# Splitting the first load of a stream-bound kernel: 512 columns ahead of 15,872

## The chip, the cores and the metric

One core of a Trainium2 chip. The metric is the time of one execution in device microseconds; most executions of a kernel here agree within 0.3%.

## The reference

```python
def reference(x, y, axis):                 # x, y: 1024 x 4096 float32, axis = -1
    return np.sum((x - y) ** 2, axis=axis).astype(np.float32)
```

33.55 MB are read, 4 KB written.

## The kernel before

Each of the 128 partitions holds eight whole rows, 32,768 columns of x and of y. Both are loaded in pieces that get smaller towards the end. VectorE subtracts, ScalarE squares and sums, and the last piece is squared and summed on VectorE.

```python
xv = x.rearrange("(p r) d -> p (r d)", p=P)      # one partition: 128 KB in a row
xw = [16384, 8192, 3072, 2688, 1312, 768, 352]   # columns of each x load
yw = [15648, 8192, 3072, 2688, 1312, 768]        # and of each y load
# ... (pieces of y are also cut out at the end: 736 and 352 columns)

def load(landed, src, dst, name, c0, c1):
    sem = tc.alloc_semaphore("%s%d" % (name, len(landed)))
    nc.sync.dma_start(out=dst[:, home(c0, c1)], in_=src[:, c0:c1]).then_inc(sem, 16)
    landed.append(((c0, c1), sem))

# order: each y load behind as much x as it needs
todo = list(order)
for _ in range(2):
    load(*todo.pop(0))               # the first two loads ...
prog.early(mybir.EngineType.SP)      # ... go out ahead of the start barrier
while todo and todo[0][5] <= H:      # H: 24,576 columns fit the buffers
    load(*todo.pop(0))
# ... compute; later loads wait until ScalarE has freed a row
```

All loads go out from one queue, SP's, and one load runs on all 16 DMA engines: eight partitions, hence eight packets, for each.

Of the kernel before, what the change touches and what calls it, by code (L numbers as in the profile page):

```python
# [52 lines left out]
def kernel(tc, x, y, axis, out):  # L53
# [21 lines left out]



    xw = [16384, 8192, 3072, 2688, 1312, 768, 352]
    yw = [15648, 8192, 3072, 2688, 1312, 768]
    late, last = 736, 352  # L80
    LATE = 3
# [201 lines left out]
```

## Time and profile before

| | before |
|---|---|
| time, median (3 runs) | 86.06 us (86.02 to 86.10) |
| span of the profiled run | 84.1 us |
| VectorE / ScalarE busy | 43% / 38% |
| DMA engines' share | 94.1% |

Three more lines of the kernel before: the packet count from the page and, from the timeline (start, length, engine, instruction), the last subtractions and the store.

```profile
DMA packets 2304, 33.56 MB, mean 399 GB/s; under 512 B 384, under 2 KB 640, under 8 KB 1280
```

```profile
78.52 2.34 DVE L172 TENSOR_TENSOR X<-X,Y 128x768 f32<-128x768 f32 x3 [0.26 <-DMA Y<-in_y_dram]
...
81.71 0.35 SPq L245 DMA_DIRECT2D out_dram<-results  x1
```

VectorE still waits for data at 78.52 us, and the store goes out 3.2 us later: the end hangs on the stream of loads.

The packet count is 2,048 packets of data (15 loads and the store, 128 each) and 256 completion records of 4 bytes, one per engine and transfer.

### The profile page before, as it was taken

How to read it: one execution, taken by the hardware profiler on the slowest of the kernel's cores; microseconds unless marked ns; L12 is line 12 of the kernel's file. 1: busy time of each engine (PE TensorE's matmuls, PEld its weight loads, DVE VectorE, ACT ScalarE, POOL GpSimd, SP SyncE). 2: the span in 40 equal slices, each digit the busy share in tenths (PEclk: the TensorE clock that was granted, in tenths of full speed). 3: DMA queues.
4: the chain of work that ended last, by engine and by line, in shares of the span. 5: the costliest groups of instructions: out<-in, count | busy, mean ns of one | idle time of the engine just before them, and what ended most of it. 6: DMA issues, size and time to landing. Idle time of an engine off the chain costs nothing.

```text
span 84.1 us, 110 instructions
## 1 busy us (share of the span) xinstructions
DVE 36.3 (43%) x17; ACT 31.6 (38%) x26; POOL 0.2 (0%) x4
## 2 busy tenths in 40 slices
DVE  0000000000000000000899999990699999199870
ACT  4200000000000000000007979799505979997980
POOL 0000000000000000000000000000000000000000
DMA  9479999992999999995899979996999999999900
GB/s 499 187 312 499 499 499 499 499 436 92 447 476 476 476 476 476 476 476 249 358 390 499 499 327 421 499 452 296 438 421 438 424 424 425 400 424 412 363 0 2
DMA packets 2304, 33.56 MB, mean 399 GB/s; under 512 B 384, under 2 KB 640, under 8 KB 1280
## 3 DMA queue, kind: packets, MB, share of 16 engines
q1 hardware_dynamic: 2304, 33.56, 94.1%
HBM read 33.55 MB, written 0.00 MB: 399 GB/s over the span
## 4 chain that ended last, share of the span: by engine, by line
DMA 71%; DVE 14%; ACT 10%; SPq 1%; issue 0%
DMA Y<-in_y_dram 71%; DVE X L172 14%; ACT X L178 10%; SPq L114 1%; ACT results L219 0%
## 5 line engine op out<-in xcount | busy, mean ns | idle before, releaser
L172 DVE TENSOR_TENSOR X<-X,Y 128x4096 f32<-128x4096 f32 (+8 forms) x13 | 35.6, 2781 | 45.2 <-DMA Y<-in_y_dram 45.1
L178 ACT ACTIVATE X<-X 128x4096 f32<-128x4096 f32 (+7 forms) x12 | 29.4, 2449 | 48.7 <-DVE X L172 48.7
L178 ACT ACTIVATION_READ_ACCUMULATOR X<-X 128x1 f32 x12 | 2.2, 186 | 0.0
L178 ACT ACT_TABLE_LOAD x1 | 1.3, 1283 | 1.3 <-PEq L264 1.3
L202 DVE CUSTOM_DVE_ANT_0 Y<-X,head 128x352 f32<-128x352 f32 x1 | 0.6, 583 | 0.1
L219 ACT ACTIVATE results<-parts 128x1 f32<-128x1 f32 x1 | 0.3, 294 | 0.0
L196 DVE TENSOR_REDUCE head<-parts 128x1 f32<-128x3 f32 x1 | 0.1, 150 | 0.0
L235 DVE TENSOR_REDUCE results<-parts 128x1 f32<-128x2 f32 x1 | 0.1, 147 | 0.0
L264 POOL MEMSET const-bfloat16-1.0<- 128x1 bf16 x1 | 0.1, 102 | 0.0
L264 POOL MEMSET const-uint8-127<- 128x1 uint8 x1 | 0.1, 102 | 0.0
L264 POOL MEMSET const-float32-0.0<- 128x1 f32 x1 | 0.1, 99 | 0.2 <-issue 0.2
L264 POOL MEMSET const-float32-1.0<- 128x1 f32 x1 | 0.1, 99 | 0.0
L202 DVE DVE_READ_ACCUMULATOR2_ANT results<- 128x1 f32 x1 | 0.1, 81 | 0.0
## 6 DMA issues: line engine op xcount, KB each, us to landing
Y<-in_y_dram SPq DMA_DIRECT2D x1, 7824.0 KB, 39.8
X<-in_x_dram SPq DMA_DIRECT2D x1, 4096.0 KB, 48.6
Y<-in_y_dram SPq DMA_DIRECT2D x1, 4096.0 KB, 58.0
X<-in_x_dram SPq DMA_DIRECT2D x1, 1536.0 KB, 14.9
Y<-in_y_dram SPq DMA_DIRECT2D x1, 1536.0 KB, 18.2
X<-in_x_dram SPq DMA_DIRECT2D x1, 1344.0 KB, 17.5
Y<-in_y_dram SPq DMA_DIRECT2D x1, 1344.0 KB, 20.4
X<-in_x_dram SPq DMA_DIRECT2D x1, 656.0 KB, 21.5
```

The lines of the kernel that those rows point to most:

```text
L114: nc.sync.dma_start(out=dst[:, home(c0, c1)], in_=src[:, c0:c1]).then_inc(sem, 16)
L172: nc.vector.tensor_sub(out=a, in0=a, in1=Y[:, home(c0, c1)]).then_inc(diffs, 1)
L178: nc.scalar.activation(out=a, in_=a, func=Square, accum_out=acc).then_inc(acts, 1)
L196: nc.vector.tensor_reduce(out=head, in_=parts_of(r, len(row_parts[r]) - 1), axis=mybir.AxisListType.X, op=add).then_inc(sums, 1)
L202: nc.vector.tensor_tensor_reduce(out=Y[:, home(*piece)], in0=X[:, home(*piece)], in1=X[:, home(*piece)], scale=1.0, scalar=head, op0=mult, ...
L219: nc.scalar.activation(out=results[:, r : r + 1], in_=b, func=Identity, bias=a).then_inc(acts, 1)
L235: nc.vector.tensor_reduce(out=results[:, r : r + 1], in_=parts_of(r, len(row_parts[r])), axis=mybir.AxisListType.X, op=add,).then_inc(sums, 1)
L264: nc = _bacc.Bacc("TRN2", target_bir_lowering=False, num_devices=1)
```

## The change

The intent, as the size suggests: small packets (2 KB a row instead of 64 KB) should get the stream moving sooner. The diff is one line:

```diff
-    xw = [16384, 8192, 3072, 2688, 1312, 768, 352]
+    xw = [512, 15872, 8192, 3072, 2688, 1312, 768, 352]
```

Because exactly two loads go out ahead of the barrier, the second part of x also takes the early place that the first y load had.

## The prediction

> **What bounds the kernel now.** I read the page first, then the start and the end of the timeline, the table by stages, and the packet records of the trace one by one. The page's busy shares and its slices:
>
> ```profile
> span 84.1 us, 110 instructions
> DVE 36.3 (43%) x17; ACT 31.6 (38%) x26; POOL 0.2 (0%) x4
> ...
> DMA  9479999992999999995899979996999999999900
> ...
> q1 hardware_dynamic: 2304, 33.56, 94.1%
> ```
>
> No compute engine is busy for half of the span; the DMA engines are for 94.1% of it. The dips in the row of slices come from booking long packets in whole slices. The table by stages has columns for the stretch, its length, each engine's busy time, clock, DMA share and GB/s:
>
> ```profile
> 0.00:1.00 1.00, 0.00 (x0) 0.00 (x0) 0.20 (x4) 1.00 0.00 0
> 1.00:40.00 39.00, 0.00 (x0) 1.28 (x1) 0.00 (x0) 1.00 1.02 434
> ...
> 59.00:73.00 14.00, 12.03 (x3) 9.30 (x7) 0.00 (x0) 1.00 1.00 424
> 73.00:80.00 7.00, 6.10 (x6) 6.39 (x9) 0.00 (x0) 1.00 0.98 395
> ```
>
> One unbroken stream from 1.00 to about 80 us. The packet records confirm it: each of the 16 engines moves one packet at a time, each starting where the last ended, with no hole from 1.00 to 79.91 us, and the last load's count is complete at 80.31 us. What follows is fixed: the last subtraction, the fused square and sum, and the store. So **the time is the moment at which the stream starts moving, plus its transfer time, plus a fixed tail**.
>
> The chain of waits seems to say something else and needs care:
>
> ```profile
> 40.21 8.77 DVE X L172 x2
> 48.98 0.02 issue
> 49.01 3.72 ACT X L178 x2
> 52.73 0.02 issue
> 52.74 0.33 SPq L114
> 53.07 0.04 issue
> 53.11 20.36 DMA Y<-in_y_dram
> ```
>
> It goes through compute because the issue at 52.74 waited for a freed buffer. But the first packet of that load (10,752 bytes each) started at 66.21 us: the load stood in the queue for 13 us behind earlier ones. Compute in the middle has that much slack; only the queue counts.
>
> The start, which the change touches:
>
> ```profile
> 0.00 0.38 SPq L114 DMA_DIRECT2D X<-in_x_dram  x1
> ...
> 0.43 0.42 SPq L114 DMA_DIRECT2D Y<-in_y_dram  x1
> ...
> 1.26 0.33 SPq L114 DMA_DIRECT2D X<-in_x_dram  x1
> 1.64 0.52 SPq L114 DMA_DIRECT2D Y<-in_y_dram  x1
> ```
>
> The first issue takes 0.38 us and its first packet is recorded at 1.00 us. The first round of 16 packets of 65,536 bytes then takes 3,109 ns on average (2,596 to 3,316), all later rounds of that size 2,419 ns: the start loses 0.69 us besides the first empty 1.00 us. That is all that a change of the first packets could win. Fifteen engines start between 1.00 and 1.31 us and lose 0.56 to 0.90 us; one starts at 1.78 and loses 0.18. So the loss depends on the moment rather than on the packet: real flow begins about 1.65 to 2.06 us on every engine (ends at 4.07 to 4.48, less 2.42).
>
> **What the Trainium skill says.** "DMA: Bandwidth & Descriptors", section Specifications, puts the ceiling of the 16 engines at 435 GB/s and the first byte of a hardware-generated DMA at about 0.6 us. The trace agrees with both: 16 x 65,536 bytes in 2.419 us are 433 GB/s, and from the end of the first issue (0.38) to the first packet (1.00) is 0.62 us. The stream therefore runs at its ceiling and no shape of packet raises it. The same page, "Why small descriptors are slow", tells of a fixed overhead of about 3 cycles per packet. The trace shows such a constant: the median packet is 2,420 ns for 65,536 bytes, 1,213 for 32,768, 460 for 12,288, 121 for 3,072 and 60 for 1,408. From the first two the slope is 1,207 / 32,768 = 0.03683 ns per byte; what is left over is 6, 6, 7, 8 and 8 ns. "Perfetto Trace Analysis", section DMA Optimizations, warns that DMAs under 2 KB pay significantly per transfer; here the 1,408-byte packets of the tail pay 8 of 60 ns, and 2,048 bytes sit at the edge. The first page's section "Latency and other measured facts" has HBM access at 0.2 us on average and 2 us under high load; the 0.69 us lies between, but no record here shows what it consists of.
>
> **The change part by part.** The order of instructions per engine is the same on all but SP, which has one DMA more: x in 512 columns, x in 15,872, then y in 15,648.
>
> Bytes stay: 33.56 MB, 0 us. Packets rise by 128 (one per partition) from 2,304 to 2,432, which is 8 more per engine. A row of 65,536 bytes (2,420 ns) becomes one of 2,048 bytes, 0.03683 x 2,048 + 8 = 83 ns, and one of 63,488, 0.03683 x 63,488 + 6 = 2,344 ns: together 2,427, or 7 ns more. Eight rows make 8 x 7 = 0.06 us per engine on the path. One completion record of some 9 ns more per engine makes it 0.07.
>
> Issue: the first one should still take about 0.38 us, since its length doesn't follow the size (0.33 to 0.52 for loads of 4 to 8 MB), so the first packet comes at 1.00 again. The second part of x takes y's early place at 0.43 and reaches the engines about 1.43. The small packets last until 1.65 + 8 x 0.083 = 2.3 us on the earliest engine, so no hole: spare 0.9 us. Y now goes out behind the barrier at about 1.26 and is needed when x ends at 21 us: 19 us to spare, no cost. All later issues slip by one place, some 0.4 us, against 20 us of queue.
>
> Start loss of 0.69 us: I choose to leave it as it is. An engine that can't get data before about 1.65 to 2.06 us can't get it in small packets either, and the read wait is then paid once, in the first packet or spread over the first few. Change: 0.
>
> VectorE waits for one semaphore more before its first subtraction. That count will be complete near 1.65 to 2.06 + 0.66 + 0.35 (the delay from last packet to landing, 21.39 to 21.74 in this trace) = 2.7 to 3.1 us, against 40.2 us, and the middle has slack: 0 us.
>
> Sum: +0.07 us. Last landing 80.31 to 80.38, span 84.1 to about 84.2, time 86.06 to 86.13, rounded to **86.1 us**.
>
> **The rivals.** (A) The slow first round belongs to the large packet, for example 16 engines reading long bursts at once from a standstill; small first packets would take the edge off, and the big ones would follow with their reads already under way. For it: only the first round is slow, and the shift to y at 21 us, as cold an input as x was, costs nothing (2,309 ns from its first round on) because it starts behind running packets. Against it: the engine that began latest lost least with the same 64 KB packet. At the most it wins the 0.69 less 0.07, 0.6 us, giving 85.5; half of it gives 85.8. I give it 15 to 20%.
>
> (B) Small packets from a standstill each expose part of the read wait, or many rows at one column offset hit the same part of the memory. Against it: in the tail five loads of 3,072 down to 1,408 bytes per row, all 128 rows at one offset with the same 128 KB pitch, run at exactly the rate of the fit, to the nanosecond. They had running reads ahead, though. If the eight packets took 0.1 us more each, the loss would be up to 0.8 us where nothing hides it; since the big packets' reads are queued by 1.43 us I expect 0.3 at most: 86.4. About 15%.
>
> (C) The second issue comes too late and the engines stand empty between the two parts. It would take more than the spare 0.9 us; under 5%, and it would cost the size of the hole.
>
> (D) Hidden anyway: the end is set by compute. It is not: VectorE waits 0.26 us for a load at 78.52, and the final pieces wait for their landings, so any shift of the stream passes to the end in full.
>
> **Range and chances.** The three runs spread over 0.08 us. Around 86.1 I put 0.35 down for A at half strength (85.75) and 0.3 up for B (86.4). Two per cent is 1.72 us, more than twice the whole start loss, and no single step above reaches it upwards either: within 2% in 97 of 100, the rest split for a state of the stream that I can't see.
>
> **What would show it.** Packets 2,432 in the queue's row. First packet at 1.00; 2,048-byte packets at a median of 83 ns except the first of each engine, which carries the 0.6 to 0.9 us; then 2,344 ns for the 63,488-byte ones without a slow first round; no hole; first y packet near 21.0 to 21.5 us (before 20.98 to 21.39); last landing near 80.4. I am wrong if the y packets start before 20.8 (A), if the small packets stay slow beyond the first (B), if a gap stands ahead of the large ones (C), or if later rounds leave 433 GB/s.

## The result, and the profile after

| | before | after |
|---|---|---|
| time, median (4 runs each) | 86.04 us (85.94 to 86.10) | 85.98 us (85.78 to 86.09) |
| span of the profiled run | 84.1 us | 84.3 us |

Ratio 0.9992, 95% interval 0.9971 to 1.0013: the same. A ratio is the mean time of one kernel's fast runs over the mean of the other's of the same rounds, so not quite the ratio of the medians. Later rounds on one chip gave 1.0006 (0.9988 to 1.0023).

The page of the changed kernel: its span, DMA slices, packets and queue.

```profile
span 84.3 us, 111 instructions
...
DMA  9499999994799999995969997997999999999800
...
DMA packets 2448, 33.56 MB, mean 398 GB/s; under 512 B 400, under 2 KB 656, under 8 KB 1424
...
q1 hardware_dynamic: 2448, 33.56, 93.8%
```

144 packets more: the 128 that the prediction counted, and 16 completion records that it costed but left out of the count. The bytes are unchanged. The table by stages (stretch, length, busy times, clock, DMA share, GB/s) shows the same unbroken stream:

```profile
0.00:1.00 1.00, 0.00 (x0) 0.00 (x0) 0.20 (x4) 1.00 0.01 2
1.00:40.00 39.00, 0.00 (x0) 1.28 (x1) 0.00 (x0) 1.00 1.02 433
...
59.00:73.00 14.00, 12.03 (x3) 9.27 (x7) 0.00 (x0) 1.00 1.00 425
73.00:80.00 7.00, 5.88 (x6) 6.39 (x9) 0.00 (x0) 1.00 0.96 388
```

The start and the end of the timeline after the change:

```profile
0.00 0.85 SPq L114 DMA_DIRECT2D X<-in_x_dram  x2
...
1.26 0.33 SPq L114 DMA_DIRECT2D Y<-in_y_dram  x1
```

```profile
78.74 2.33 DVE L172 TENSOR_TENSOR X<-X,Y 128x768 f32<-128x768 f32 x3 [0.24 <-DMA Y<-in_y_dram]
...
81.94 0.35 SPq L245 DMA_DIRECT2D out_dram<-results  x1
```

Both x loads are issued by 0.85 us, y goes out behind the barrier at 1.26, and the end of the kernel has moved by 0.22 us (78.52 to 78.74) and 0.23 us (81.71 to 81.94). In the chain of waits the first y load now appears from its later issue, which saves nothing: it lands at 40.39 us against 40.19 before.

```profile
1.26 39.14 DMA Y<-in_y_dram
40.39 0.02 issue
40.42 8.77 DVE X L172 x2
```

The share and the slices can't show the start in enough detail, so I summed the packet records of the trace. Per engine, from 1.00 us (the first packet) to its first y packet, the time is: lateness and gaps, the packets' own time at their median, and what they took above their median. The part that isn't the median is the start loss. Averages over the 16 engines, in us; the last columns give the mean and the last of the 16 moments at which an engine reaches y, and the span:

```
                 late,  excess,       excess,          loss   y mean  y last   span
                 gaps   first x part  15,872 cols etc.
before           0.13   0.68 (64 KB)      -            0.82   21.19   21.39   84.09
before, again    0.23   0.68 (64 KB)      -            0.91   21.28   21.64   84.36
after            0.09   0.27 (2 KB)      0.35          0.71   21.13   21.61   84.31
after, again     0.17   0.15 (2 KB)      0.45          0.78   21.20   21.94   84.66
```

Two readings. First, the mean loss is about 0.1 us smaller after the change, and the extra packets, at their medians (eight of 84 and eight of 2,342 ns for eight of 2,420, and one more completion record of 9), take 0.06 us of that back: the engines reach y 0.05 to 0.08 us earlier on average. Second, the span follows the last engine, not the mean: in these four profiles it is 62.70, 62.72, 62.70 and 62.72 us behind the last engine's first y packet. Every engine carries the same bytes at the same rate, so one that starts 0.4 us late ends 0.4 us late. The last engine varied from 21.39 to 21.94 us, more than the mean moved.

### The profile page after: what moved, and what is told of

Its sections match the earlier page's. It is cut to its first block, busy times and chain, and to the rows that moved or that the text cites. A ratio compares the mean times of both kernels' runs of the same rounds, so it can differ in the third digit from the quotient of the medians.

```text
span 84.3 us, 111 instructions
## 1 busy us (share of the span) xinstructions
DVE 36.3 (43%) x17; ACT 31.6 (38%) x26; POOL 0.2 (0%) x4
## 2 busy tenths in 40 slices
DMA packets 2448, 33.56 MB, mean 398 GB/s; under 512 B 400, under 2 KB 656, under 8 KB 1424
## 3 DMA queue, kind: packets, MB, share of 16 engines
q1 hardware_dynamic: 2448, 33.56, 93.8%
## 4 chain that ended last, share of the span: by engine, by line
DMA 71%; DVE 14%; ACT 10%; SPq 0%; issue 0%
DMA Y<-in_y_dram 71%; DVE X L172 14%; ACT X L178 10%; SPq L114 0%; ACT results L219 0%
```

## The experiments

Eleven runs were made, nine of them of new kernels. The theories: *moment* (the loss belongs to the first microsecond after the launch), *standstill* (16 engines that start together lose some 0.7 us, whenever that is), *disturbance* (the later loads' issues slow the first packets), *lockstep* (the engines read the same offsets of rows a power of two apart), and the cost of 7 to 8 ns per packet.

### The two kernels again

No edit. These are the second profiles in the table above; the changed kernel was also timed in five rounds.

> The changed kernel again, unchanged, for a second profile and a closer interval. First theory (the slowest engine decides): the start loss is a matter of the moment at which each of the 16 engines gets its data, it differs from run to run, and the mean over the engines is about 0.05 us earlier at the first y packet than in the kernel before while the last engine is up to 0.2 us later: ratio 0.997 to 1.003, and in the profile the span follows the last engine's first y packet (span about 62.70 us after it), not the mean. Second theory (the small packets cost 0.07 us each time and win nothing): last y packet start always about 0.07 later than before's 21.39, ratio 1.0008.

Measured: 86.10 us (85.90 to 86.44, 6 runs) against 85.96 (85.86 to 86.16, 11 runs), ratio 1.0006 (0.9988 to 1.0023). The profiled run was the slow end, 86.44 us, and its store went out at 82.29 us:

```profile
82.29 0.35 SPq L245 DMA_DIRECT2D out_dram<-results  x1
```

That is 0.35 us behind the 81.94 of the first profile. The last engine's first y packet came at 21.94 us against 21.61, 0.33 us later, while the mean rose by only 0.07. The packet records show why: that engine ended its small packets at 1.84 us and began its first large one only at 2.62, though the load had been issued by 0.85. It stood empty for 0.79 us while each of the others went from one part to the other without a pause, and without that hole it would not have been the last: the next one reached y at 21.40. The first profile has no such hole. The first theory's "0.05 earlier on average, last engine later" held (the last engine even more than the 0.2 us given for it); the second theory's fixed +0.07 us did not.

> The kernel before again, for a second profile of its start. If the start is as described, the first round of 65536-byte packets averages 3.0 to 3.15 us and the engines' first y packets average 21.15 to 21.25 us with the last at 21.35 to 21.65; the mean repeats within 0.05 us and the last engine does not.

Measured: 86.14 us, one run, whose state is unknown. First round 3,109 ns, the same figure as in the first profile; the mean over the engines 21.28, 0.09 us later than in the first profile, so it repeats less well than the 0.05 us I expected, because the first packets were later (0.23 against 0.13 us); last engine 21.64.

### The small piece in mid-stream

```diff
-    xw = [512, 15872, 8192, 3072, 2688, 1312, 768, 352]
+    xw = [15872, 512, 8192, 3072, 2688, 1312, 768, 352]
```

The load order becomes x 15,872, y 15,648, x 512, and so on. (The expectation's "2432" should read 2,448, by the same slip as in the prediction.)

> The same pieces with the small one second: x in 15872 columns first, then y, then 512 columns of x. Same bytes, same 2432 packets of inputs, but the kernel starts with a large packet as before. If the cost per packet is what the prediction took (8 more packets per engine at 7 to 8 ns and a completion record of 9 ns), the stream ends 0.07 us later than before's: 86.1, ratio 1.0008, with a slow first round of about 3.0 us (2.34 plus 0.69). If small packets at the start are what wins time, this one lacks the win and is 0.1 to 0.2 us slower than the changed kernel; if the start loss is the same for both, they are equal within 0.1 us. Small packets in mid-stream should be 84 ns each with none slower.

Measured: 86.02 us (86.02 to 86.07, 5 runs), ratio 1.0003 (0.9991 to 1.0015). The first round of 63,488-byte packets took 3,061 ns against 2,344 later, an excess of 0.72 us. The 2 KB packets at 39 us took 84 ns, none of them slow, and the 32 KB packets of the x load behind them 1,213. So the step from small to large packets costs nothing in a running stream; and with the small piece moved away from the start, the time is within 0.1 us of the changed kernel's.

### Only x issued at the start

A VectorE memset on a part of Y that is loaded later holds back y and all that follows.

```diff
-    for _ in range(2):
-        load(*todo.pop(0))
+    load(*todo.pop(0))               # twice in the version of the changed kernel
     prog.early(mybir.EngineType.SP)
+    go = tc.alloc_semaphore("go")
+    nc.vector.memset(Y[:, 0:4096], 0.0)
+    nc.vector.memset(Y[:, 4096:8192], 0.0).then_inc(go, 1)
+    nc.sync.wait_ge(go, 1)
```

> The kernel before with only the first x load issued at the start; y and everything later waits for a VectorE memset of some microseconds (y is needed only at 21 us, so nothing starves). Theory 'disturbance' (the descriptors of the loads issued at 0.43 to 2.2 us slow the first round): first round falls from 3.1 to about 2.5 us, y starts at 20.5 to 20.8 us, time about 85.5, ratio 0.993. Theory 'moment' or 'large packets from a standstill': first round stays 3.0 to 3.2 us, y at 21.0 to 21.4 us, time within 0.15 us of before.

The timeline of this version of the kernel before shows that y was issued only at 9.47 us:

```profile
5.97 3.47 DVE L130 MEMSET Y<- 128x4096 f32 x1 [0.80 <-issue]
9.47 0.33 SPq L114 DMA_DIRECT2D Y<-in_y_dram  x1
```

Measured: 86.08 us (86.06 to 86.12, 5 runs), ratio 1.0008 (0.9996 to 1.0020). First round 2,996 ns against 3,109: 0.11 us less, not the 0.6 of the disturbance theory. The round under way while the held loads were issued took 2,453 ns instead of 2,419, so issues seem to cost a little, 0.03 us here. Loss 0.84 us, y 21.21 on average, last 21.61.

> The changed kernel with only the two x parts issued at the start and the rest held back by the same memset. Its first large packets took 2.49 to 2.97 us, 0.36 us over their later 2.34 on average. Theory 'disturbance': they fall to about 2.4 us, the small ones lose their slow ones too, last y start near 21.0, time about 85.5. Theory 'moment': small ones stay slow until about 1.6 us and the large ones' first round stays near 2.7: time within 0.15 us of the changed kernel.

Measured: 85.89 us (85.87 to 86.02, 5 runs), ratio 0.9989 (0.9977 to 1.0001). Excess 0.18 us in the small packets and 0.25 in the large ones, loss 0.63 us, the smallest of all, but most of it is still there; last engine 21.39. The median is 0.21 us below that of the changed kernel in the same rounds (86.10), more than the 0.15 allowed; those six runs spread over 0.54 us. Disturbance may carry 0.1 to 0.15 us of the loss; in the time neither kernel shows it clear of noise.

### A second start

```diff
-    for _ in range(2):
-        load(*todo.pop(0))
+    load(*todo.pop(0))
     prog.early(mybir.EngineType.SP)
+    nc.sync.wait_ge(landed_x[0][1], 16)
```

> The changed kernel, but the large part of x is issued only after the small part has landed (about 2.6 us), so the engines stand still and then start a second time, with memory and engines already used. Theory 'cold' (the start loss is paid once, by whatever comes first after the launch): first packet of the large part at about 3.7 us, first round at 2.34 to 2.45 us, first y packets at 22.4 to 22.7, time about 87.2. Theory 'standstill' (16 engines that start together lose 0.7 us, whenever it is): the first round of 63488-byte packets takes about 3.0 us again, first y packets at 23.1 to 23.5 us, time about 87.9.

The table by stages of this run shows the gap: no packet starts between 2.20 and 3.40 us.

```profile
1.00:2.20 1.20, 0.00 (x0) 1.07 (x1) 0.00 (x0) 1.00 0.66 219
2.20:3.40 1.20, 0.00 (x0) 0.00 (x0) 0.00 (x0) 1.00 0.00 0
3.40:4.40 1.00, 0.00 (x0) 0.00 (x0) 0.00 (x0) 1.00 3.09 1016
```

(A long packet is booked where it starts, hence 1,016 GB/s in the last line.) Measured: 87.94 us (87.90 to 88.17, 4 runs), ratio 1.0216 (1.0186 to 1.0247). The large packets began at 3.49 us, and their first round took 3,094 ns on average (2,778 to 3,319), the later ones 2,343: an excess of 0.75 us, at engines and memory that had just been used. The y packets began at 23.10 on average. That is the standstill theory's number in each place (3.0 us, 23.1 to 23.5, 87.9) and rules out the moment theory: **the loss was paid again at a second common start of the 16 engines.**

### The addresses

The first x load reads with a row pitch of 130,048 bytes. A recalculation of what it computes gives errors of up to 11%, over 0.1% in 492 of the 1,024 sums; the comparison with the reference let them pass.

```diff
-        nc.sync.dma_start(out=dst[:, home(c0, c1)], in_=src[:, c0:c1])...
+        part = src[:, c0:c1]
+        if name == "x" and c0 == 0:
+            part = bass.AP(part.tensor, part.offset, [[32512, P], [1, c1 - c0]])
+        nc.sync.dma_start(out=dst[:, home(c0, c1)], in_=part)...
```

> Wrong result on purpose: the kernel before, but the first x load reads rows that lie 130,048 bytes apart in memory instead of 131,072, so that neighbouring engines (four rows apart) start 4 KB out of step in the memory's addresses; sizes, packets and order are unchanged. Theory 'lockstep' (16 engines reading the same offsets of rows a power of two apart slow each other until they have drifted out of step): the first round falls from 3.0-3.1 to at most 2.6 us, and the spread of the engines shrinks; the loss may come back when y starts in step at 21 us. Theory 'not the addresses': first round stays at 2.9 to 3.2 us, y from 21.0 to 21.6, time within 0.15 us of before.

Measured: 86.76 us (86.52 to 86.85, 6 runs), ratio 1.0069 (1.0047 to 1.0091): a miss for both theories. The first round averaged 3,117 ns, as before, so putting neighbouring engines 4 KB out of step did not lessen the loss. But it ranged from 2,658 to 3,925 ns, and the last engine reached y at 22.03 us with a mean of 21.16. The store in the timeline:

```profile
82.34 0.35 SPq L248 DMA_DIRECT2D out_dram<-results  x1
```

0.63 us behind the 81.71 of the kernel before, as the last engine is (22.03 less 21.39 is 0.64). With these addresses the loss fell more unequally on the engines in the one profile, and the unluckiest engine set the time; that the other five runs (86.69 to 86.85 us) have the same cause is likely, not shown. Why this pitch is worse stays open.

### Eight small loads, at the start and in mid-stream

```diff
-    xw = [512, 15872, 8192, 3072, 2688, 1312, 768, 352]
+    xw = [512] * 8 + [12288, 8192, 3072, 2688, 1312, 768, 352]    # at the start
+    xw = [12288] + [512] * 8 + [8192, 3072, 2688, 1312, 768, 352]  # mid-stream
```

> Eight loads of 512 columns ahead of one of 12288, so the cost per packet is taken seven times more. By the prediction's term: a row of x is 8 packets of 83 ns and one of 1816, together 2483 ns against 2420, 63 ns more; eight rows 0.51 us and eight completion records of 9 ns 0.07: first y packets on average 0.58 us later than the 21.19 of before, or about 0.46 later if small packets at the start also win the 0.12 us seen in the changed kernel. Time about 86.5 (86.4 to 86.6), ratio 1.005 to 1.007. Rival: if small packets at the start win more the longer they last (large packets are slow whenever they come within the first 2 to 5 us), the first round of the 49152-byte packets is at full rate, 1816 ns, and the time is 86.2. Rival the other way: small packets from SP come too slowly (0.4 us of issue for each 0.67 us of data), holes, over 87.

Measured: 88.06 us (87.71 to 88.62, 4 runs), ratio 1.0229 (1.0190 to 1.0268). My number was wrong by a factor of three to four. The timeline of this run gives the nine x issues in one merged line:

```profile
0.00 4.42 SPq L114 DMA_DIRECT2D X<-in_x_dram  x9
```

0.49 us an issue, all done by 4.42 us, while the last small packets ran until 8.6. So the rival's time was right, and its reason in part: although SP was on the whole ahead of the data, there was a hole.

```profile
1.20:2.40 1.20, 0.00 (x0) 1.16 (x1) 0.00 (x0) 1.00 1.01 355
2.40:3.60 1.20, 0.00 (x0) 0.12 (x1) 0.00 (x0) 1.00 0.67 183
```

From 2.40 to 3.60 us the DMA engines were busy for 67% only, and by the packet records 7.3 of the 16 had no packet under way, on average, from 2.6 to 3.3. That is where the first two small loads end and the third is due, which was issued by 1.57 us, the first behind the barrier. The small packets themselves were slow, too, 101 ns on average against a median of 84, single ones up to 1,228 ns: 1.10 us of excess per engine, and 0.42 us of lateness and gaps.

> The partner of the run with eight small loads first: 12288 columns of x first, then the eight loads of 512, so the same bytes and packets, but the small ones run behind a large load and their descriptors are queued long before. Prediction's term: 7 to 8 ns per packet and 9 ns per completion record, 0.58 us in all: time 86.6 (86.4 to 86.8), ratio 1.005 to 1.009, small packets 84 ns with almost none slower. Rival (small packets are slower wherever they stand): mean packet about 101 ns as before, 1.5 us or more lost, 87.5 or above.

Measured: 86.69 us (86.60 to 86.81, 4 runs), ratio 1.0076 (1.0062 to 1.0091), or 0.65 us against the 0.58 of the sum. Mean small packet 85 ns. The same packets with a large load ahead of them, issued long before they are due, cost what the prediction's term says; right behind a standstill they cost three times that. Part of that is the hole, part the slow packets; why the third load's packets came late and what the slow ones wait for, the records don't tell.

### A first part of 4,096 columns

```diff
-    xw = [512, 15872, 8192, 3072, 2688, 1312, 768, 352]
+    xw = [4096, 12288, 8192, 3072, 2688, 1312, 768, 352]
```

> One size changed: the first part of x has 4096 columns (16 KB packets, 607 ns each at the stream's rate) instead of 512. Theory 'standstill' (every engine loses 0.7 to 0.8 us in all on its way to full rate, whatever the packets): summed over all packets the loss from 1.00 us on is 0.65 to 0.85 us per engine, most of it in the first one or two packets of 16 KB, none in the large ones that follow 4.9 us later; mean first y packet 21.1 to 21.25, time 85.9 to 86.2. Rival 'large packets pay on their first round whatever ran before': first round of 49152-byte packets 1.95 us or more instead of 1.815, mean first y packet above 21.3.

Measured: 85.92 us (85.88 to 86.31, 6 runs), ratio 0.9998 (0.9980 to 1.0016). The first 16 KB packet of each engine took 1,177 ns against 611 later, the second 636, the third 626; the 49,152-byte packets 1,815 from their first round on. Loss 0.73 us, y 21.16 on average, last 21.39. The standstill theory holds: what the packets lose sits in the first three rounds of 16 KB and the large ones pay nothing, which also refutes the rival.

### Two queues

```diff
-    def load(landed, src, dst, name, c0, c1):
+    def load(landed, src, dst, name, c0, c1, queue=nc.sync):
...
-        nc.sync.dma_start(out=dst[:, home(c0, c1)], in_=src[:, c0:c1])...
+        queue.dma_start(out=dst[:, home(c0, c1)], in_=src[:, c0:c1])...
...
-    for _ in range(2):
-        load(*todo.pop(0))
+    load(*todo.pop(0))
     prog.early(mybir.EngineType.SP)
+    load(*todo.pop(0), nc.scalar)
+    prog.early(mybir.EngineType.Activation)
```

> The kernel before with the first y load issued by ScalarE's queue at the start beside SP's first x load, so that every DMA engine has two queues to serve from its first packet on. If what is lost at a standstill is waiting that a second queue can fill, the mean loss falls from 0.8 to 0.4 us or less and the time to about 85.6, ratio 0.995: a version that beats both. If the loss belongs to the engine, not to the queue, it stays: time within 0.15 us of before. Packets of x and y should alternate, both loads landing near 40 us, which the first subtraction doesn't mind.

The page of this run shows two queues at work:

```profile
q1 hardware_dynamic: 2160, 25.55, 72.1%
q10 hardware_dynamic: 144, 8.01, 22.0%
```

Measured: 86.01 us (85.90 to 86.39, 6 runs), ratio 1.0000 (0.9983 to 1.0017). First round 3,197 ns, then x and y packets alternate at 2,418 and 2,310. A second queue doesn't shorten the loss.

No version beat both kernels clear of noise; the best ratio is the 0.9989 of the changed kernel with the later loads held back, and its interval reaches 1.

## Why the prediction was right, point by point

**The bound** (right). The stream runs from 1.00 to 40 us at 434 and 433 GB/s, and with its smallest packets, from 73 to 80 us, at 395 and 388; the end follows it by a fixed tail. What the prediction did not have: the end follows the last of 16 engines. Its sum was one for the average engine, and the average moved by -0.05 to -0.08 us while the last engine of single runs moved by several tenths. The range of 85.75 to 86.4 held because these tenths are what it allowed for its rivals. That the time also fell next to the 86.1 us is partly luck: the rise of 0.07 us was not there, and the scatter of the runs (0.2 to 0.5 us) is larger than it.

**Packets, +0.07 us** (right). 84 ns for 2,048 bytes and 2,342 for 63,488 were measured, 83 and 2,344 predicted; with the completion record that makes 0.06 us. The term taken eight times cost 0.65 us against 0.58 in mid-stream. It holds only for a queue that is already running.

**Issue, early place, y behind the barrier, VectorE's wait** (right but for one engine). The first packet came at 0.99 us, and y was never late: with everything but x held back until 9.5 or 9.9 us the times did not rise by more than 0.12 us. But the early place with 0.9 us to spare did not always keep the second part of x on time: in the second profile of the changed kernel it began on one engine only at 2.62 us, 0.79 us after the small packets had ended there.

**"Start loss: change 0"** (nearly right in size, wrong in reason). The prediction counted 0.69 us, the first round alone; with late starts the mean went from 0.82 and 0.91 us to 0.71 and 0.78. But the prediction said that the loss belongs to the moment, that flow can't begin before 1.65 to 2.06 us, and that the wait is paid once by the small packets. The second start at 3.5 us refutes the first part: 0.75 us lost again. Nor did the flow wait until 1.65 us: in the changed kernel single 2 KB packets took 81 ns, their full rate, from 1.05 us on, beside others of up to 436 ns. The changed kernel's own packets refute the last: 2 KB packets ran at 84 ns on most engines from about 1.6 us on, yet the first round of large packets took 2,487 to 2,966 ns, 0.35 us above its median on average. A small first packet does not pay off the loss, it takes a part of it and hands the rest on; a first part in 16 KB packets pays it all.

**The rivals.** A (small packets win up to 0.6 us) is the direction of the mean, at 0.1 us; the large packets did not "follow with their reads already under way". B (each small packet exposes a wait) shows with one small load in single packets (34 of the 128 took over 90 ns, more than one per engine) but not in the time, and is very visible with eight: the chance I gave it belonged to a larger dose. C (a hole between the parts) did not occur in the first profile, but did in the second, on one of the 16 engines: 0.79 us, and as that engine became the last, about 0.5 us of that run's time. D (compute hides it) did not occur.

**Left open.** What the 0.7 us of a standstill consists of; addresses, second queue and later issues make little of its mean. Whether the 16 engines must start together for it: the one that began its large packets alone at 2.62 us took 2,933 ns for the first (0.59 too long), while in the kernel before the one that began at 1.78 us took 2,596 (0.18 too long). Why the spread of the engines changes from run to run; in one profile the late second part explains it, but two profiles of each kernel are too few to say that the change widens it.

## What to carry to other kernels

When a kernel's end is a DMA stream at its ceiling, changing the shape of the first packets can win only the start loss, here 0.6 to 0.9 us, and each form of the start tried here kept most of it. Ask for the last of the 16 engines, not for the average, and keep the queue from ever standing still: the one restart tried cost 0.75 us besides the gap. Keep small packets behind a large load and issue them long before they are due; there 2 KB ones cost the fit's few nanoseconds each. At the start, in number, they cost three times that, and even one small first load leaves its successor little time: one late engine is enough to lose what it could win.

## What the Trainium skill lacked or had wrong

- "DMA: Bandwidth & Descriptors" gives the first byte of a hardware-generated DMA (0.62 us here, agreeing), but nothing on what follows it: a common start of all 16 engines lost another 0.4 to 0.8 us in the packets themselves, and again after a gap of over 1 us. Nor does it say how far the engines differ: a load issued by 0.85 us left one of them empty from 1.84 to 2.62 us.
- Of the pace of the slowest engine "DMA: Bandwidth & Descriptors" speaks only for a load beside other traffic. No page that I read says that engines keep the delay of their start to the end of a stream of loads, so that the last engine sets the time: spans of 62.69 to 62.77 us behind its first y packet in ten profiles, with a last engine 0.20 to 0.88 us behind the mean.
- The section "Why small descriptors are slow" of "DMA: Bandwidth & Descriptors" and the section DMA Optimizations of "Perfetto Trace Analysis" speak of a cost per packet or transfer. For 2 KB packets it depends on the queue: 85 ns on average and +0.76% for eight loads behind a large one, 101 ns and +2.29% for the same eight at the start.
- The section "Latency and other measured facts" of "DMA: Bandwidth & Descriptors" lists row pitches of 512 KiB and more that lower the rate. Here a pitch of 127 KiB instead of 128 left the rate and the mean loss alone, and the kernel still took 0.69% longer, in the profiled run through the spread of the engines, which no page has.
